# The order of the three partial products in every large matrix product of a two-layer hybrid backbone

## The chip, the core and the metric

The kernel runs on one core of one Trainium2 chip. A core has several engines with a program of their own each: TensorE (PE, matrix products; its weight loads are listed apart as PEld), VectorE (DVE), ScalarE (ACT), GpSimd (POOL) and SyncE (SP, which here starts the transfers). They meet through semaphores. The metric is the device time of one execution in microseconds, the median over several runs.

## What is computed

The reference passes 256 latent tokens and 256 context tokens of width 1024 through two layers. Layer 0 mixes with a state-space head group and a retention group that share one input and one output projection, layer 1 with an mLSTM block; each is followed by a SwiGLU feed-forward part (FFN), and the end is an RMSNorm. All in float32.

```python
def swiglu(h, w1, w3, w2):
    return (jax.nn.silu(h @ w1) * (h @ w3)) @ w2

def block_update(x, y, mod, ffn_norm_w, w1, w3, w2):
    x = x + (mod[2] * y).astype(x.dtype)
    hf = modulate(rmsnorm(x, ffn_norm_w), mod[3], mod[4])
    return x + (mod[5] * swiglu(hf, w1, w3, w2)).astype(x.dtype)
...
    for layer in range(DEPTH):
        ...
            y_l, _ = ssd_retention_mixer(h_l, rope, st, *p)
        ...
            y_l, _ = mlstm_mixer(h_l, st, *p)
        lat = block_update(lat, y_l, mod_l, norm_ffn_w[layer], ffn_w1[layer], ffn_w3[layer], ffn_w2[layer])
    return rmsnorm(lat, final_norm_w)
```

Most of the work is large products of activations (up to 512 tokens) with weight matrices: the input projections, the FFNs' three products, the mLSTM's up and down projections.

## The kernel before

TensorE multiplies tiles in the type fp32r. To keep more of float32's digits, each operand of a large product is split in two: a high part H, the operand cast to fp32r, and a low part L, what the cast left over. A product is then the sum of three partial products, high by high, high by low and low by high, accumulated in one PSUM tile.

The parts come from two engines. For a weight tile of 128x1024 SP loads wraw (L355; up to three are loaded ahead), ACT casts it to wH (L367), and VectorE subtracts to make wL (L227, the line of a helper that records every two-operand operation). wH and wL have four buffers each; `wnext` keeps up to three pairs ready. For an activation tile ACT writes hH (L499) and VectorE hL (L500); in the FFN's middle the pair is uH (L1144) and uL (L227 again). Tiles with names such as hp, hHL, uHL and yHL hold both parts in one tile, so that both read alike in a view.

`mm3` (L401) issues the partial products. It gets pairs ((lh, ll), (rh, rl)): lh and ll are the high and low part of the operand that is loaded into the array (stationary, `lhsT`), rh and rl those of the operand that streams through it (moving, `rhs`). For outputs of 512 columns it runs over two halves of 256, `CT_` and `LT_`; for each half it goes over all pairs (the 128-row slices of the contraction), and for each pair it issues three matmuls of 128x256, at L409, L410 and L411. In the trace's names `mm<-hL,wH` the moving tile stands first, the stationary one second.

Nearly everywhere the weight is stationary. In `projB`, whose output has tokens on its rows, the activation is stationary and the weight moves, so there the low moving part is wL. `mm3` is called from the first stage (L595), which makes the normalised input h slice by slice while it multiplies, from `projA` and `projB`, `out_quarter`, `tail_tiles` and `head_tiles` (FFN0 begins with several tiles at once, slice by slice), `ffn0`, `ml_qkv` (the mLSTM's blockwise projections of the convolved xc), `ztile`, `down`, and the last FFN.

Only SP's program stands in the order in which it is written. For the other engines a scheduler places the instructions by its own estimate of when their inputs and buffers are ready, so their rows can differ from the order in the source, and a changed line can move rows on engines that it doesn't name.

Of the kernel before, what the change touches and what calls it, by code (L numbers as in the profile page):

```python
# [186 lines left out]
def tile_hybrid(ctx, tc, A, out, dbg=None):  # L187
    nc = tc.nc
    V, S, G, TE = nc.vector, nc.scalar, nc.gpsimd, nc.tensor
# [14 lines left out]
    def s2(p="s2", shape=(P, 512), dt=F32):  # L204
        return sb.tile(list(shape), dt, tag="s2", name=nm(p), bufs=36)
# [195 lines left out]
    def mm3(o, pairs, first=True, last=True):  # L401

        n = len(pairs)
        if o.shape[-1] > 256:
            for sl in (CT_, LT_):
                mm3(o[:, sl], [(lp, cols(rp, sl)) for lp, rp in pairs], first and sl is CT_, last and sl is LT_)
            return
        for i, ((lh, ll), (rh, rl)) in enumerate(pairs):
            TE.matmul(o, lhsT=lh, rhs=rh, start=first and i == 0, stop=False)  # L409
            TE.matmul(o, lhsT=lh, rhs=rl, start=False, stop=False)  # L410
            TE.matmul(o, lhsT=ll, rhs=rh, start=False, stop=last and i == n - 1)  # L411

    def wk(w, k, n=P, o=0):

# [2 lines left out]
    def cols(hl, sl):  # L417
        return tuple(t[:, sl] for t in hl)
# [156 lines left out]
    for i, k in enumerate(seq):  # L575
        ld(i + 3)
        wload()
        if i < 4:
            if i > 0:
                wprep()  # L580
            w4.append(wready.pop(0))
        if i == 0:
            xn = h_a(k, rb, amix[0], ALL)
        h_b(hs[k], k, xn, mod[0][0], ALL)
        if i == 0:
            prep(1)
        prep(i + 2)
        TE.matmul(pdt[0:32, :], lhsT=wdt[:, k, :], rhs=hs[k](ALL)[0], start=i == 0, stop=False)
        TE.matmul(pdt[0:16, :], lhsT=wdt[:, k, 0:16], rhs=hs[k](ALL)[1], start=False, stop=i == KD - 1)
        if i + 1 < KD:  # L590
            fin(i + 1)
            xn = h_a(seq[i + 1], rb, amix[0], ALL)
        for j, w in enumerate(w4):
            for n in range(i + 1) if j == i else (i,):
                mm3(p4[j], [(wk(w, seq[n]), hs[seq[n]](ALL))], n == 0, n == KD - 1)  # L595
    nc.sync.dma_start(out=rowp, in_=A["rowp"][0].partition_broadcast(P))
    rl = rowp[:, RC["retl"]:RC["retl"] + 8]
# [104 lines left out]
    def projA(hs):  # L702
        w = wnext()
        p = mmps()
        for sl in (CT_, LT_) if hs[0].packed else (ALL,):
            mm3(p[:, sl], [(wk(w, k), hs[k](sl)) for k in range(KD)])
        return p

    def projB(hs, evac):
        ws = [wnext(), wnext()]  # L710
        for c in range(NCH):
            p = mmps([P, 256])
            sl = slice(c * P, (c + 1) * P)
            mm3(p, [(hs[k](sl), tuple(ws[k // 4][z][:, (k % 4) * 256:(k % 4 + 1) * 256] for z in range(2)))
                    for k in range(KD)])
            evac(c, p)
            slot()
# [705 lines left out]
    for op in order.split():  # L1423
        n = done[op] = done.get(op, -1) + 1
# [67 lines left out]
    for m in range(KD):  # L1492
        o = s2("fin")[:, :256]
# [22 lines left out]
```

## Time and profile before

| what | value |
|---|---|
| three runs | 1354.46, 1344.43, 1341.25 us |
| their median | 1344.43 us |
| the profiled execution's own time | 1343.85 us |
| its span, from the first to the last instruction | 1341.9 us |
| mean granted TensorE clock | 0.987 |
| PE / PEld / DVE / ACT / POOL busy | 1305.2 / 1250.5 / 947.8 / 642.1 / 125.0 us |

Busy time is the time in which at least one instruction of the engine ran. Matmuls are pipelined: one lasts about 0.28 us by the profile, while the next starts 0.11 to 0.12 us after it. So the time of a run of matmuls is read from the distances of their starts, or from how many a window holds. A wait belongs to the instruction that waited, and the profile names what came last for it.

### The profile page before, as it was taken

Reading aid. Unit: us, or ns where it says so; the run is one execution under the profiler, and the core shown is the slowest. Engines: PE = TensorE matmul, PEld = TensorE weight load, DVE = VectorE, ACT = ScalarE, POOL = GpSimd, SP = SyncE. Lnnn points to the kernel's source line nnn. Section 1 sums busy time; section 2 is a strip of 40 time slices with the busy share of each in tenths; the row PEclk is TensorE's granted clock in tenths of the full one; section 3 lists DMA queues with packets and bytes.
Section 4 is the critical chain, followed back from the end, with each engine's and each line's share of the span. In section 5 each row is a group of like instructions: output and inputs, shape, how many; then the busy total and the mean of one; then the engine's idle time right before and its main releaser. Section 6 shows DMA issues by size and latency. Waiting matters only on the chain.

```text
span 1341.9 us, 25691 instructions
## 1 busy us (share of the span) xinstructions
PE 1305.2 (97%) x10510; PEld 1250.5 (93%) x10510; DVE 947.8 (71%) x1703; ACT 642.1 (48%) x1114; POOL 125.0 (9%) x138
## 2 busy tenths in 40 slices
PE   7999999999999999999999999989999999999997
PEld 4899999989999999999999999989999689999997
DVE  7888787966876567897557643586666897666555
ACT  4366757846864243222322132465556563544443
POOL 0022031311021030000000310300000000000001
PEclk9999999999999999999999999999999999899998
DMA  9337344434412225567557633412124434465553
GB/s 369 111 143 236 122 162 142 134 126 152 148 48 88 80 94 188 178 237 244 190 189 249 213 95 97 140 63 63 48 65 145 138 101 146 129 206 198 194 193 122
DMA packets 60855, 201.00 MB, mean 150 GB/s; under 512 B 6841, under 2 KB 8377, under 8 KB 60737
## 3 DMA queue, kind: packets, MB, share of 16 engines
q1 hardware_dynamic: 60594, 199.36, 44.8%
q8 instruction: 82, 1.34, 0.4%
q14 instruction: 35, 0.29, 0.1%
q10 hardware_dynamic: 144, 0.01, 0.0%
HBM read 197.16 MB, written 1.13 MB: 148 GB/s over the span
## 4 chain that ended last, share of the span: by engine, by line
PE 69%; DVE 13%; issue 7%; DMA 5%; ACT 3%; POOL 1%; SPq 0%; POOLq 0%; DVEq 0%; ACTq 0%
PE mm L410 20%; PE mm L409 20%; PE mm L411 20%; DVE wL L227 3%; DVE junk L267 3%; DMA ada<-in_ada 2%; PE sc L958 1%; ACT wH L367 1%; DMA erow<-scr 1%; PE mm L1219 1%; DVE junk L291 1%; PE sc L840 1%; DVE conv L687 1%; DVE comb L227 1%; DMA wraw<-in_wup 1%
## 5 line engine op out<-in xcount | busy, mean ns | idle before, releaser
L367 ACT CAST wH<-wraw 128x1024 fp32r<-128x1024 f32 x248 | 259.4, 1048 | 408.0 <-PE mm L410 236.3
L227 DVE TENSOR_TENSOR wL<-wraw,wH 128x1024 fp32r<-128x1024 f32 x248 | 306.2, 1236 | 144.0 <-ACT wH L367 134.2
L410 PE MATMUL mm<-hL,wH 128*128 128x256 f32 x1088 | 303.1, 279 | 0.7 <-DVE hL L500 0.7
L409 PE MATMUL mm<-hH,wH 128*128 128x256 f32 x1088 | 299.5, 279 | 2.8 <-ACT hH L499 2.1
L411 PE MATMUL mm<-hH,wL 128*128 128x256 f32 x1088 | 301.8, 279 | 0.0
L409 PEld LDWEIGHTS mm<-hH,wH 128*128 128x128 f32 x1088 | 204.3, 190 | 4.5 <-ACT hH L499 2.8
L410 PEld LDWEIGHTS mm<-hL,wH 128*128 128x128 f32 x1088 | 205.7, 189 | 2.0 <-DVE hL L500 1.7
L411 PEld LDWEIGHTS mm<-hH,wL 128*128 128x128 f32 x1088 | 205.5, 189 | 0.5
L267 DVE SCALAR_TENSOR_TENSOR junk<-ada,cbc 128x1024 bf16<-128x1024 f32 x128 | 158.2, 1236 | 22.1 <-DMA ada<-in_ada 20.2
L409 PE MATMUL mm<-wH,hH 128*128 128x256 f32 x384 | 110.2, 287 | 0.2 <-ACT conv L684 0.2
L409 PE MATMUL mm<-hp,wH 128*128 128x256 f32 x384 | 108.6, 287 | 0.1
L410 PE MATMUL mm<-hp,wH 128*128 128x256 f32 x384 | 108.2, 284 | 0.0
L410 PE MATMUL mm<-wL,hH 128*128 128x256 f32 x384 | 108.0, 282 | 0.1
L411 PE MATMUL mm<-hp,wL 128*128 128x256 f32 x384 | 108.1, 283 | 0.0
L411 PE MATMUL mm<-wH,hL 128*128 128x256 f32 x384 | 107.4, 280 | 0.0
L983 DVE SCALAR_TENSOR_TENSOR xt<-mm,mod,xt 128x256 f32<-128x256 f32 x144 | 64.5, 478 | 59.3 <-PE mm L411 58.9
L687 DVE SCALAR_TENSOR_TENSOR conv<-xp,prm,conv 128x512 f32<-128x512 f32 x128 | 96.2, 754 | 12.5 <-ACT conv L684 10.9
L410 PE MATMUL mm<-uL,wH 128*128 128x256 f32 x352 | 98.2, 279 | 0.7 <-DVE uL L227 0.7
L409 PE MATMUL mm<-hHL,wH 128*128 128x256 f32 x352 | 97.6, 279 | 1.1 <-ACT hHL L499 1.1
L409 PE MATMUL mm<-uH,wH 128*128 128x256 f32 x352 | 97.8, 279 | 0.6 <-ACT uH L1144 0.6
L410 PE MATMUL mm<-hHL,wH 128*128 128x256 f32 x352 | 97.8, 278 | 0.0
L411 PE MATMUL mm<-hHL,wL 128*128 128x256 f32 x352 | 97.8, 278 | 0.0
(329 smaller groups left out, 3105.1 us busy)
## 6 DMA issues: line engine op xcount, KB each, us to landing
wraw<-in_f SPq DMA_DIRECT2D x136, 512.0 KB, 4.2
ada<-in_ada SPq DMA_DIRECT2D x80, 512.0 KB, 5.0
wraw<-in_win SPq DMA_DIRECT2D x48, 512.0 KB, 4.4
wraw<-in_wup SPq DMA_DIRECT2D x32, 512.0 KB, 3.5
erow<-scr SPq DMA_DIRECT2D x16, 512.0 KB, 7.1
wraw<-in_wout SPq DMA_DIRECT2D x16, 512.0 KB, 4.0
wraw<-in_wdn SPq DMA_DIRECT2D x16, 512.0 KB, 3.5
adaf<-in_ada SPq DMA_DIRECT2D x10, 512.0 KB, 7.6
```

Source lines behind the costliest of these rows:

```text
L227: eng.tensor_tensor(out=o, in0=a, in1=b, op=op)
L267: V.scalar_tensor_tensor(out=junk, in0=raw, scalar=1.0, in1=cbc[:, st, :], op0=ALU.mult, op1=ALU.mult, accum_out=mod[l][c][:, k, st:st + 1])
L291: V.scalar_tensor_tensor(out=junk, in0=raw, scalar=1.0, in1=cbc[:, st, :], op0=ALU.mult, op1=ALU.mult, accum_out=to)
L367: S.copy(out=H, in_=raw)
L409: TE.matmul(o, lhsT=lh, rhs=rh, start=first and i == 0, stop=False)
L410: TE.matmul(o, lhsT=lh, rhs=rl, start=False, stop=False)
L411: TE.matmul(o, lhsT=ll, rhs=rh, start=False, stop=last and i == n - 1)
L687: V.scalar_tensor_tensor(out=o, in0=x[:, :, k:k + 256], scalar=pc(wname, t * 5 + k), in1=o, op0=ALU.mult, op1=ALU.add)
L840: TE.matmul(p1[:, i, h * 64:(h + 1) * 64], lhsT=comb[(g, c0 + i)][:, h, :], rhs=xtok[:, c0 + i, h * 64:(h + 1) * 64], start=True, stop=True)
L958: TE.matmul(py[:, i, :], lhsT=src[:, i * P:(i + 1) * P], rhs=vt[:, j, :], start=j == 0, stop=j == len(srcs) - 1)
L983: V.scalar_tensor_tensor(out=xt[:, m, half], in0=p[:, o:o + 256], scalar=gate[:, m, st:st + 1], in1=xt[:, m, half], op0=ALU.mult, op1=ALU.add)
L1219: TE.matmul(pv[:, c, :], lhsT=xm[:, c0 // 2, 2 + c * P:2 + (c + 1) * P], rhs=b[:, P:], start=True, stop=True)
```

## The change

In `mm3`, the second and the third partial product change places. The first stays high by high; then comes low stationary by high moving, then high stationary by low moving. The accumulation's last matmul, which carries `stop`, is now the latter.

```diff
@@ -407,8 +407,8 @@
             return
         for i, ((lh, ll), (rh, rl)) in enumerate(pairs):
             TE.matmul(o, lhsT=lh, rhs=rh, start=first and i == 0, stop=False)
-            TE.matmul(o, lhsT=lh, rhs=rl, start=False, stop=False)
-            TE.matmul(o, lhsT=ll, rhs=rh, start=False, stop=last and i == n - 1)
+            TE.matmul(o, lhsT=ll, rhs=rh, start=False, stop=False)
+            TE.matmul(o, lhsT=lh, rhs=rl, start=False, stop=last and i == n - 1)
```

The lines keep their numbers, so L410 of before is L411 of after and the other way round. PE has as many rows as before; the scheduler moves rows on PE, ACT and VectorE beyond the exchange. Three places follow.

The first is PE's row at the head of FFN0, where four output tiles (numbers 5806, 5807, 5808 and 6021 at the end of their names) start on the first slice of h. Before:

```order
L409 MATMUL mm_829_5806<-hH_772_5587,wH_788_5603 128x256
L409 MATMUL mm_830_5807<-hH_772_5587,wH_791_5609 128x256
L409 MATMUL mm_831_5808<-hH_772_5587,wH_815_5766 128x256
L409 MATMUL mm_855_6021<-hH_772_5587,wH_818_5774 128x256
L410 MATMUL mm_829_5806<-hL_773_5588,wH_788_5603 128x256
L411 MATMUL mm_829_5806<-hH_772_5587,wL_789_5604 128x256
```

After:

```order
L409 MATMUL mm_829_5806<-hH_772_5587,wH_788_5603 128x256
L410 MATMUL mm_829_5806<-hH_772_5587,wL_789_5604 128x256
L409 MATMUL mm_830_5807<-hH_772_5587,wH_791_5609 128x256
L410 MATMUL mm_830_5807<-hH_772_5587,wL_792_5610 128x256
L409 MATMUL mm_831_5808<-hH_772_5587,wH_815_5766 128x256
L410 MATMUL mm_831_5808<-hH_772_5587,wL_816_5767 128x256
L409 MATMUL mm_855_6021<-hH_772_5587,wH_818_5774 128x256
L410 MATMUL mm_855_6021<-hH_772_5587,wL_819_5775 128x256
L411 MATMUL mm_829_5806<-hL_773_5588,wH_788_5603 128x256
```

The first matmul that reads hL was the fifth of this stretch and is the ninth. In the same way, where a part of FFN0's down product ends on its last uL, one more matmul stands ahead of it than before: line 410 of the last product, beside its line 409 and two matmuls of the next tile.

The second place is ACT's and VectorE's row at the first convolution of the mLSTM, whose result xcH feeds the blockwise projections. ACT before:

```order
L367 CAST wH_1393_10312<-wraw_1363_10132 128x1024
L682 COPY xp0_645<-mm_1365_10136 128x2x256
L684 ACTIVATE conv_1386_10292<-mm_1365_10136,prm_68 128x512
L682 COPY xp1_646<-mm_1366_10137 128x2x256
L367 CAST wH_1415_10428<-wraw_1364_10134 128x1024
```

ACT after:

```order
L682 COPY xp0_645<-mm_1365_10136 128x2x256
L684 ACTIVATE conv_1386_10292<-mm_1365_10136,prm_68 128x512
L367 CAST wH_1393_10312<-wraw_1363_10132 128x1024
L682 COPY xp1_646<-mm_1366_10137 128x2x256
L367 CAST wH_1415_10428<-wraw_1364_10134 128x1024
```

VectorE at the same place, before:

```order
L227 TENSOR_TENSOR wL_1394_10313<-wraw_1363_10132,wH_1393_10312 128x1024
L687 SCALAR_TENSOR_TENSOR conv_1386_10292<-xp0_645,prm_68,conv_1386_10292 128x512 x2
L227 TENSOR_TENSOR wL_1416_10429<-wraw_1364_10134,wH_1415_10428 128x1024
L687 SCALAR_TENSOR_TENSOR conv_1386_10292<-xp0_645,prm_68,conv_1386_10292 128x512
L227 TENSOR_TENSOR gm_10278<-mm_1404_10388,rowp_69 128x32
L687 SCALAR_TENSOR_TENSOR conv_1386_10292<-xp0_645,prm_68,conv_1386_10292 128x512
```

VectorE after:

```order
L687 SCALAR_TENSOR_TENSOR conv_1386_10292<-xp0_645,prm_68,conv_1386_10292 128x512 x2
L227 TENSOR_TENSOR wL_1394_10313<-wraw_1363_10132,wH_1393_10312 128x1024
L687 SCALAR_TENSOR_TENSOR conv_1386_10292<-xp0_645,prm_68,conv_1386_10292 128x512
L227 TENSOR_TENSOR gm_10278<-mm_1404_10388,rowp_69 128x32
L687 SCALAR_TENSOR_TENSOR conv_1386_10292<-xp0_645,prm_68,conv_1386_10292 128x512
```

The cast of the weight tile has moved behind the copy and the first tap of the convolution on ACT; on VectorE the first wL has moved behind two further taps, and the second (10429, further down) behind all of them.

The third place is VectorE's row in the second head of the mLSTM's scan, where earg (12078, 12096) is scaled at L1331 before PE reads it at L1338. Before:

```order
L1329 RECIPROCAL rr_1672_12082<-rr_1672_12082 128x2
L227 TENSOR_TENSOR rr_1677_12100<-rr_1677_12100,den_1674_12091 128x2
L1318 ISA earg_1699_12208,negm_1696_12202<-urow_1695_12199,mmask_1382_10283 128x512
L1318 ISA negm_1696_12202 128x1
L1329 RECIPROCAL rr_1677_12100<-rr_1677_12100 128x2
L227 TENSOR_TENSOR wL_1712_12272<-wraw_1688_12158,wH_1711_12271 128x1024
L1331 SCALAR_TENSOR_TENSOR earg_1671_12078<-earg_1671_12078,rr_1672_12082,earg_1670_12074 128x512
```

After:

```order
L1329 RECIPROCAL rr_1677_12100<-rr_1677_12100 128x2
L1318 ISA earg_1699_12208,negm_1696_12202<-urow_1695_12199,mmask_1382_10283 128x512
L1318 ISA negm_1696_12202 128x1
L1331 SCALAR_TENSOR_TENSOR earg_1671_12078<-earg_1671_12078,rr_1672_12082,earg_1670_12074 128x512
L1321 SCALAR_TENSOR_TENSOR earg_1698_12204,den_1697_12203<-earg_1698_12204,S_1539_11242 128x512
L1331 SCALAR_TENSOR_TENSOR earg_1676_12096<-earg_1676_12096,rr_1677_12100,earg_1675_12092 128x512
```

wL_1712_12272 no longer stands ahead of the first L1331; it comes some ten rows behind it. On PE the matmul that reads earg_12078 has moved forward too: of the matmuls of lines 409 to 411 for tile 12277, ten follow it now, where two followed it before.

## Rows read from the trace of the kernel before

**Rows 1.** The page, part 1: busy us (share of the span) x instructions.

```profile
PE 1305.2 (97%) x10510; PEld 1250.5 (93%) x10510; DVE 947.8 (71%) x1703; ACT 642.1 (48%) x1114; POOL 125.0 (9%) x138
```

**Rows 2.** The page, part 4: the chain that ended last, shares by engine.

```profile
PE 69%; DVE 13%; issue 7%; DMA 5%; ACT 3%; POOL 1%; SPq 0%; POOLq 0%; DVEq 0%; ACTq 0%
```

**Rows 3.** Windows: us, busy (x instructions) by engine, granted clock, DMA share, GB/s.

```profile
585.20:715.20 130.00, 130.00 (x1150) 130.00 (x1149) 89.28 (x146) 33.47 (x40) 0.00 (x0) 1.00 0.62 211
716.00:828.00 112.00, 112.00 (x952) 111.98 (x952) 58.95 (x88) 27.99 (x35) 14.50 (x16) 1.00 0.49 163
1154.00:1332.00 178.00, 178.00 (x1573) 178.00 (x1572) 106.56 (x136) 84.13 (x118) 5.16 (x5) 1.00 0.56 181
490.00:503.00 13.00, 12.61 (x95) 12.41 (x96) 12.34 (x30) 5.97 (x14) 0.94 (x2) 0.87 0.30 116
```

**Rows 4.** The page, part 5: weight loads by line; busy, mean ns, then idle before.

```profile
L409 PEld LDWEIGHTS mm<-hH,wH 128*128 128x128 f32 x1088 | 204.3, 190 | 4.5 <-ACT hH L499 2.8
L410 PEld LDWEIGHTS mm<-hL,wH 128*128 128x128 f32 x1088 | 205.7, 189 | 2.0 <-DVE hL L500 1.7
```

**Rows 5.** Line 410: its idle time by releaser, and who waited for it (us, times).

```profile
  DVE hL L500: 2.4, 6
  DVE uL L227: 2.0, 5
  DVE wL L227: 0.3, 1
...
  ACT wH L367: 236.3, 105
```

**Rows 6.** Timeline of PE at 491 and 715 us: start, duration, then idle before.

```profile
491.03 0.70 PE L409 MATMUL mm<-hH,wH 128*128 128x256 f32 x4
492.01 0.58 PE L410 MATMUL mm<-hL,wH 128*128 128x256 f32 x1 [0.28 <-DVE hL L500]
...
715.30 0.28 PE L410 MATMUL mm<-uL,wH 128*128 128x256 f32 x1
715.78 0.38 PE L410 MATMUL mm<-uL,wH 128*128 128x256 f32 x1 [0.21 <-DVE uL L227]
```

**Rows 7.** Timeline of PE in the middle of FFN0's second down product.

```profile
750.87 0.28 PE L409 MATMUL mm<-uH,wH 128*128 128x256 f32 x1
750.99 0.28 PE L410 MATMUL mm<-uL,wH 128*128 128x256 f32 x1
751.10 0.28 PE L411 MATMUL mm<-uH,wL 128*128 128x256 f32 x1
751.22 0.28 PE L409 MATMUL mm<-uH,wH 128*128 128x256 f32 x1
751.34 0.28 PE L410 MATMUL mm<-uL,wH 128*128 128x256 f32 x1
```

**Rows 8.** Timelines of ACT, DVE and PE before the mLSTM's first blockwise product.

```profile
879.14 1.05 ACT L367 CAST wH<-wraw 128x1024 fp32r<-128x1024 f32 x1 [1.54 <-PE mm L410]
...
880.22 1.23 DVE L227 TENSOR_TENSOR wL<-wraw,wH 128x1024 fp32r<-128x1024 f32 x1 [2.10 <-ACT wH L367]
...
882.85 1.22 DVE L227 TENSOR_TENSOR wL<-wraw,wH 128x1024 fp32r<-128x1024 f32 x1
...
887.22 0.39 PE L409 MATMUL mm<-xcH,bH 128*128 128x256 f32 x1 [4.31 <-ACT xcH L1200]
887.44 0.40 PE L1229 MATMUL sc<-xcH,ghl 128*32 128x512 f32 x1
887.95 0.58 PE L410 MATMUL mm<-xcL,bH 128*128 128x256 f32 x1
```

**Rows 9.** Timelines of DVE and PE in the mLSTM scan's second head.

```profile
1041.98 1.21 DVE L227 TENSOR_TENSOR wL<-wraw,wH 128x1024 fp32r<-128x1024 f32 x1
1043.11 1.41 DVE L1331 SCALAR_TENSOR_TENSOR earg<-earg,rr,earg 128x512 f32<-128x512 f32 x2
...
1044.00 0.63 PE L1338 MATMUL sc<-cst,earg 128*128 128x128 f32 x4 [2.30 <-DVE earg L1331]
```

## Prediction, made before the changed kernel ran

> **What bounds the kernel now.** I read the engines' busy shares first. TensorE (PE) is busy 97% of the span, and it executes as many weight loads (PEld) as matmuls, 10510 each [rows 1]; VectorE follows with 71%. The chain of work that ended last says the same: 69% of it is PE [rows 2]. So the time is a count of matmuls times their spacing, plus the short stretches in which PE stands still, and a change that only permutes matmuls can act on the spacing or on the stretches.
>
> For the spacing I read windows in which PE never idles. From 585.2 to 715.2 us 1150 matmuls take 130 us, 113.0 ns each, and from 1154 to 1332 us 1573 take 178 us, 113.2 ns each. From 716 to 828 us, with the same granted clock of 1.00 and matmuls of the same shape, 952 take 112 us, 117.6 ns each [rows 3]. The reader should see two cadences at one clock, 4.5 ns apart, and that a cadence, once there, lasts over a thousand matmuls. No row tells what selects it; the slower stretch begins right behind a short stop at 715.78 us [rows 6].
>
> For the stops I read what PE waited for ahead of line 410, which before the change is the first matmul to need a low moving operand: 2.4 us in 6 waits for hL and 2.0 us in 5 for uL [rows 5]. No line 411 had a wait of that size, since whatever it needs was made before. The two largest stops elsewhere that touch rearranged code are 4.31 us for xcH [rows 8] and 2.30 us for earg [rows 9].
>
> **The change, part by part.** It adds and removes no instruction: 9408 matmuls of lines 409 to 411, counted in the program (a third each, 3136), stay, and their weight loads with them.
>
> *The kept stationary.* Before, lines 409 and 410 use one stationary twice running; after, no two neighbours of a triple share it (line 411 returns to the first). If the second load had been cheap, 3136 cheap loads would be lost. The loads' mean times are 190 ns at line 409 and 189 at line 410, where the same tile is loaded again [rows 4], and a run of five matmuls has steps of 0.12 and 0.12 into line 410, 0.11 into line 411, and 0.12 into line 409 [rows 7]: the step that repeats the stationary is not the shorter one. Cost taken: 0. Bounds: the loads differ by 1 ns, so 3136 x 1 ns = 3.1 us of loss at most by these rows; a gain of the same size isn't excluded.
>
> [...]
>
> *Waits for low parts.* The wait moves from the second matmul of a triple to the third, so one more matmul (0.113 us) runs ahead of it. At the last part of each FFN0 down product PE stops for uL, as at 715.78 us, where the step from the matmul ahead is 0.48 us instead of 0.11 [rows 6]. Ahead of that wait stood, after the triple before, line 409 of the last product and lines 409 and 410 of the next tile; now line 410 of the last product stands there too. Three such places: 3 x 0.113 = -0.34 us. At FFN0's head four matmuls of line 409 ran, and then PE waited for hL (492.01 against 491.03 us) [rows 6]; now eight run ahead of it. Four matmuls of cover: 4 x 0.113 = -0.45 us. At the first mLSTM qkv product xcL came 0.51 us after the matmul ahead of it [rows 8], and now one product of that triple and twelve of the next tile stand ahead of it: about -0.25 us, nearly all of what that step has over the one before it (0.51 - 0.22 = 0.29). The bounds for the three: 0, and all 4.4 us of waits for hL and uL [rows 5] gone. I take the direct count, since in stage one, where the other hL waits lie, the program puts as many matmuls between hH and the first use of hL as before.
>
> *Earlier use of wL, later release of wH.* wL is now needed one matmul sooner and wH is held one matmul longer (0.113 us). Work that hides it: weight pairs are made up to three tiles ahead. Ahead of line 410 PE waited for wL once, 0.3 us, while ACT's cast of wH waited for line 410 in 105 cases, 236.3 us in all [rows 5]: the casts wait for PE to free buffers, not PE for the casts. Cost 0; without that cover 0.113 us for each of the program's 248 casts, 28 us, would be the price, but this needs weights that arrive late, and the windows of the FFNs with no idle PE [rows 3] show none.
>
> *What the scheduler moves on ACT and VectorE.* Because a wH buffer now comes free only with a tile's very last matmul, ACT's reader of that tile moves ahead of the cast of the next wH. At the first mLSTM convolution ACT's cast (879.14 us, 1.05) and VectorE's two wL (880.22 us, 1.23, and 882.85 us, 1.22) ran ahead of or inside the convolution on which xcH depends [rows 8]. After, the copy and the convolution come first, and one wL is left between the steps. The chain shortens by the cast's 1.05 us, not by the sum, since the taps still follow each other; PE's wait of 4.31 us becomes about 3.26. Term: -1.05 us, bounds 0 (if another input of xcH is then last) and -2.3 (one wL more).
>
> At the mLSTM scan's second head VectorE's wL at 1041.98 us stood ahead of earg at 1043.11, 1.13 us later [rows 9]; after, it stands behind. But the matmul that reads earg also moved forward, by eight matmuls, which now run behind it (8 x 0.113 = 0.90 us). Net -0.23 us, bounds +0.9 (earg not earlier) and -1.13.
>
> **The sum.** -0.34 -0.45 -0.25 -1.05 -0.23 = -2.3 us on the profiled execution's 1343.85 us gives 1341.5. The median of the runs shown, 1344.43, is 0.6 us above that execution, so on medians 1342.1; I say 1342.0. With the bounds: gains of at most 4.4 + 2.3 + 1.1 = 7.8 us, losses of at most 3.1 + 0.9 = 4.0 us.
>
> **Rivals.**
> (a) The cadence turns long, the case on the other side. Its place: the two stretches at 113 ns, 1150 and 1573 matmuls [rows 3], each entered behind a stop whose matmul the change replaces. Its price: (1150 + 1573) x 4.5 ns = 12.3 us, so 1342 + 12.3 = 1354; the longer stretch alone 7.1 us, 1349. For it: such a stretch follows a stop directly, and every stop is rearranged. Against it: only one of three long stretches had it. Slower than before by over 1% (13.4 us) it decides only from 13.4 / 0.0045 = about 2980 matmuls on, so all of these and some of the short ones.
> (b) The cadence turns short from 716 to 828 us: 952 x 4.5 ns = 4.3 us, 1337.7. For it: that stretch's stop is shortened by one matmul; against it: nothing tells what selects it.
> (c) The kept stationary did save something: +3.1 us, 1345. Against it: equal loads and steps [rows 4, 7]. [...]
> [...]
> (e) The stops only move: whatever ends a wait ends the next at the same time, and nothing changes, 1344.4.
>
> **How the numbers follow.** The forecast (1338 to 1346, its own range, and it includes e) has 0.60; (a) 0.18, of which 0.06 reach past 1%; (b) 0.12, of which 0.04 come with so much of the waits' upper bound, 1342 - 4.3 - 5.3 = 1332 and below, that it is about 1%; (c) 0.04; (d) 0.06. The range for 8 in 10 goes from 1334 (b with part of the larger gains) to 1352 (a with its longer stretch and (d)'s wait). About 1% is what a measurement of this kernel can tell from no change: the limits are 1331.0 and 1357.9 us. Faster by more 0.05, within 0.88, slower by more 0.07.
>
> **What would show it.** Steps between starts of 113 or 117.6 ns in the same windows as before, equal for all three lines, show the cost of the kept stationary right at 0; a step into line 410 or 411 that is longer than the others shows (c). Idle ahead of line 411 for uL, three times about 0.1 us less, and hL at FFN0's head about 0.45 us less show the moved waits; a wait for xcH of about 3.3 us shows the reordered casts; 4.3 says that ACT's row wasn't its cause. Matmuls per window in the three long stretches tell (a) and (b). The prediction is wrong in its main point if steps in a stretch at full clock differ by line, or if PE gains idle of more than 4 us ahead of lines 409 to 411.

## The result and the profile after

The changed kernel is slower: 1348.96 us, the median of 20 runs (1343.63 to 1361.32), against 1341.83 us for the kernel before (20 runs, 1335.23 to 1354.46). The ratio is 1.0066, with a 95% interval of 1.0044 to 1.0088, so some 6 to 12 us were lost where 2.3 were to be gained. The ratios here and below come from the fast executions alone (those not over 1.5% above the fastest of the same kernel), and differ by up to 0.2% from the quotient of the two medians. The time lies inside the range for 8 in 10 (1334 to 1352), but above the forecast's own (1338 to 1346) and on the wrong side of the kernel before, and the loss has a cause that the sum didn't hold.

First the page of the changed kernel: part 1 (busy us, share, instructions), and from part 5 the weight loads of the three lines (busy, mean ns, then idle before).

```profile
PE 1316.3 (97%) x10510; PEld 1264.4 (93%) x10510; DVE 946.9 (70%) x1703; ACT 644.0 (47%) x1116; POOL 131.1 (10%) x138
...
L409 PEld LDWEIGHTS mm<-hH,wH 128*128 128x128 f32 x1088 | 205.1, 189 | 4.5 <-ACT hH L499 3.4
L410 PEld LDWEIGHTS mm<-hH,wL 128*128 128x128 f32 x1088 | 206.1, 189 | 0.4
L411 PEld LDWEIGHTS mm<-hL,wH 128*128 128x128 f32 x1088 | 204.4, 189 | 0.8 <-DVE hL L500 0.4
```

There is still one load for each matmul, and the loads of these groups last 189 ns at all three lines, as in [rows 4]. What the change does to TensorE's own work costs nothing that these rows show.

The waits of PE in the changed kernel (total us, times, longest) show something new at the top:

```profile
PE mm L411 <- DVE wL L227: 6.5, 3, 4.0
PE mm L409 <- ACT xcH L1200: 3.7, 1, 3.7
...
PE sc L1338 <- DVE earg L1331: 2.3, 2, 1.9
...
PE mm L411 <- DVE uL L227: 0.3, 1, 0.3
...
PE mm L411 <- DVE hL L500: 0.2, 1, 0.2
```

PE now waits 6.5 us for wL, where no matmul of the kernel before waited for one (the 0.3 us of [rows 5] is a weight load's). The waits that I had worked out did shrink: xcH from 4.31 to 3.7 us [rows 8], earg's longest from 2.30 to 1.9 [rows 9], and little is left of those for uL and hL. They are all smaller than the new one.

Here is the longest of the new stops, in the timeline of PE (start, duration, then idle before):

```profile
216.48 0.28 PE L411 MATMUL mm<-wL,hH 128*128 128x256 f32 x1
217.09 0.38 PE L409 MATMUL mm<-wH,hH 128*128 128x256 f32 x1 [0.33 <-ACT wH L367]
217.31 0.28 PE L410 MATMUL mm<-wH,hL 128*128 128x256 f32 x1
221.58 0.58 PE L411 MATMUL mm<-wL,hH 128*128 128x256 f32 x1 [4.00 <-DVE wL L227]
221.96 0.42 PE L409 MATMUL mm<-wH,hH 128*128 128x256 f32 x1
222.18 0.42 PE L410 MATMUL mm<-wH,hL 128*128 128x256 f32 x1
222.39 0.41 PE L411 MATMUL mm<-wL,hH 128*128 128x256 f32 x1
```

The names say which product this is: wH and wL stand first, so the weight moves. It is one of `projB`'s, in layer 0's mixing stage. Each of its products takes two weight tiles, and PE stands at the first low matmul of the second tile. Behind the stop the steps are 0.21 us instead of 0.11. VectorE and ACT in the same stretch show what was late:

```profile
217.06 0.74 DVE L728 SCALAR_TENSOR_TENSOR yL<-sc,prm,yH 128x512 fp32r<-128x512 f32 x1
217.73 1.40 DVE L687 SCALAR_TENSOR_TENSOR conv<-xp,prm,conv 128x512 f32<-128x512 f32 x2
219.05 0.68 DVE L227 TENSOR_TENSOR comb<-erow 128x512 f32<-128x512 f32 x1
219.65 0.74 DVE L687 SCALAR_TENSOR_TENSOR conv<-xp,prm,conv 128x512 f32<-128x512 f32 x1
220.31 1.22 DVE L227 TENSOR_TENSOR wL<-wraw,wH 128x1024 fp32r<-128x1024 f32 x1
...
213.82 1.28 ACT L757 ACT_TABLE_LOAD   x1
215.12 0.40 ACT L757 ACTIVATE erow<-erow,ncs 128x128 f32<-128x128 f32 x1
215.43 0.67 ACT L727 ACTIVATE yH<-sc,prm 128x512 fp32r<-128x512 f32 x1
216.00 1.03 ACT L367 CAST wH<-wraw 128x1024 fp32r<-128x1024 f32 x1
```

The cast of that tile ran on ACT at 216.00 us, behind the mixer's own rows, and PE's matmul at 217.09 waited 0.33 us for it. The subtraction was then ready to run, but VectorE had five other instructions in front of it (yL, three convolution taps, comb) and never idled. In the kernel before the same two instructions ran 8.5 and 9.1 us earlier, far ahead of PE, which reached this product at 217.05 us and didn't stop:

```profile
207.49 1.04 ACT L367 CAST wH<-wraw 128x1024 fp32r<-128x1024 f32 x1
...
211.24 1.22 DVE L227 TENSOR_TENSOR wL<-wraw,wH 128x1024 fp32r<-128x1024 f32 x1
```

The second stop has the same form, at another product of `projB`, 2.33 us. It is followed a little later by twelve matmuls of line 822 that take 4.44 us, where they took 2.75 before:

```profile
373.62 0.28 PE L410 MATMUL mm<-wH,hL 128*128 128x256 f32 x1
376.22 0.38 PE L411 MATMUL mm<-wL,hH 128*128 128x256 f32 x1 [2.33 <-DVE wL L227]
...
377.50 4.44 PE L822 MATMUL sc<-vw,btok 128*128 128x256 f32 x12
```

The windows (us; busy and instructions of PE, PEld, DVE, ACT, POOL; granted clock; DMA share; GB/s) price both, first of the kernel before, then of the changed one:

```profile
200.00:230.00 30.00, 29.18 (x254) 28.76 (x254) 25.36 (x37) 20.21 (x34) 2.48 (x2) 1.00 0.39 119
360.00:382.00 22.00, 22.00 (x186) 21.69 (x185) 19.60 (x35) 11.85 (x23) 0.00 (x0) 1.00 0.33 112
```

```profile
200.00:230.00 30.00, 25.68 (x199) 25.28 (x199) 23.47 (x31) 24.18 (x38) 4.00 (x4) 0.89 0.42 135
360.00:382.00 22.00, 19.67 (x147) 18.67 (x146) 19.98 (x33) 13.46 (x22) 0.00 (x0) 0.92 0.40 126
...
221.90:226.00 4.10, 4.10 (x20) 4.10 (x20) 4.10 (x7) 3.21 (x5) 0.00 (x0) 0.50 0.38 128
...
378.00:380.00 2.00, 2.00 (x7) 1.56 (x6) 1.75 (x4) 0.73 (x2) 0.00 (x0) 0.50 0.74 225
```

PE starts 55 and 39 matmuls fewer in these stretches, and the granted clock falls from 1.00 to 0.89 and 0.92. It is 0.50 in the windows behind the two stops, from 221.9 to 226.0 and from 378.0 to 380.0 us.

To follow the loss through the program, I compare the start of the same matmul of line 409 (counted from 0) in both traces. Number 406 (213.65 us before) starts 1.82 us earlier after the change and number 438 starts 5.89 us later, so the first stop costs 7.7 us. The rows give nearly all of it: the step into line 411 is 4.27 us instead of 0.11 (4.16), the one into line 409 ahead of it 0.61 (0.50), and the stretch at half clock holds 20 matmuls in 4.10 us and about 14 in the next 2 (4.10 + 2.00 - 34 x 0.113 = 2.3), with 0.27 for the step from 221.58 us. Numbers 758 to 790 span the second stop: from 2.75 to 7.25 us late, 4.5 us, of which 2.49 is the step and 4.44 - 2.75 = 1.69 line 822. Between the two 3.1 us are given back, in part by smaller waits (for `vw` 0.3 us instead of 0.8, for `zs` none instead of 0.6). By number 1014 (485 us before), the end of the mixing stage, the changed kernel is 7.2 us late.

Most of what this one execution (1358.5 us, 14.65 above the one of before) loses beyond that is cadence. These are the windows of the changed kernel that answer to [rows 3]:

```profile
593.54:718.00 124.46, 124.46 (x1058) 124.46 (x1058) 82.78 (x137) 30.12 (x36) 0.00 (x0) 1.00 0.60 199
729.60:838.00 108.40, 108.39 (x955) 108.20 (x955) 58.80 (x89) 27.96 (x35) 14.68 (x16) 1.00 0.52 168
1163.00:1338.00 175.00, 175.00 (x1488) 175.00 (x1487) 101.34 (x126) 79.37 (x111) 1.92 (x2) 1.00 0.58 183
...
490.00:503.00 13.00, 11.89 (x103) 11.67 (x102) 9.44 (x20) 6.17 (x12) 4.56 (x6) 1.00 0.34 121
```

That is 117.6, 113.5 and 117.6 ns per matmul, where [rows 3] had 113.0, 117.6 and 113.2: all three long stretches have changed sides. By the numbers, (1150 + 1573 - 952) x 4.4 ns = +7.8 us. At FFN0's head 1.1 us came back (the clock is now 1.00 there); FFN0's first stretch ran at 117.8 ns instead of 113.4 and lost 2.8; the mLSTM, where three of the forecast's terms lie, gave back 2.7. 7.2 + 7.8 - 1.1 + 2.8 - 2.7 = 14.0 us; number 3100, near the end, is 13.9 us late. Whether the cadence belongs to the change is for the experiments.

### The profile page after: what moved, and what is told of

It is laid out like the page before. It is cut to its first block, busy times and chain, and to the rows that moved or that the text cites. A ratio compares the mean times of both kernels' runs of the same rounds, so it can differ in the third digit from the quotient of the medians.

```text
span 1356.7 us, 25632 instructions
## 1 busy us (share of the span) xinstructions
PE 1316.3 (97%) x10510; PEld 1264.4 (93%) x10510; DVE 946.9 (70%) x1703; ACT 644.0 (47%) x1116; POOL 131.1 (10%) x138
## 4 chain that ended last, share of the span: by engine, by line
PE 68%; DVE 13%; issue 8%; DMA 4%; ACT 4%; POOL 2%; SPq 0%; POOLq 0%; DVEq 0%; ACTq 0%
PE mm L411 20%; PE mm L409 20%; PE mm L410 20%; DVE wL L227 3%; DMA erow<-scr 2%; DVE junk L267 2%; DVE conv L687 2%; PE sc L958 1%; DMA ada<-in_ada 1%; ACT wH L367 1%; PE mm L1219 1%; DVE junk L291 1%; PE sc L822 1%; PE sc L840 1%; DVE comb L227 1%
## 5 line engine op out<-in xcount | busy, mean ns | idle before, releaser
L409 PE MATMUL mm<-hH,wH 128*128 128x256 f32 x1088 | 304.5, 281 | 2.7 <-ACT hH L499 2.7
L410 PE MATMUL mm<-hH,wL 128*128 128x256 f32 x1088 | 303.2, 279 | 0.0
L411 PE MATMUL mm<-hL,wH 128*128 128x256 f32 x1088 | 300.5, 279 | 0.2 <-DVE hL L500 0.2
L410 PEld LDWEIGHTS mm<-hH,wL 128*128 128x128 f32 x1088 | 206.1, 189 | 0.4
L411 PEld LDWEIGHTS mm<-hL,wH 128*128 128x128 f32 x1088 | 204.4, 189 | 0.8 <-DVE hL L500 0.4
L411 PE MATMUL mm<-wL,hH 128*128 128x256 f32 x384 | 109.1, 285 | 6.5 <-DVE wL L227 6.5
L410 PE MATMUL mm<-wH,hL 128*128 128x256 f32 x384 | 108.7, 283 | 0.0
L410 PE MATMUL mm<-hp,wL 128*128 128x256 f32 x384 | 107.6, 282 | 0.0
L411 PE MATMUL mm<-hp,wH 128*128 128x256 f32 x384 | 106.8, 283 | 0.0
L409 PE MATMUL mm<-hHL,wH 128*128 128x256 f32 x352 | 100.4, 285 | 1.1 <-ACT hHL L499 1.1
L410 PE MATMUL mm<-hHL,wL 128*128 128x256 f32 x352 | 100.1, 284 | 0.0
L411 PE MATMUL mm<-hHL,wH 128*128 128x256 f32 x352 | 99.6, 284 | 0.0
L411 PE MATMUL mm<-uL,wH 128*128 128x256 f32 x352 | 97.8, 279 | 0.5 <-DVE uL L227 0.3
```

The costliest lines, as they stand in the source:

```text
L410: TE.matmul(o, lhsT=ll, rhs=rh, start=False, stop=False)
L411: TE.matmul(o, lhsT=lh, rhs=rl, start=False, stop=last and i == n - 1)
```

## The experiments

The theories. A: the order of the matmuls itself costs nothing; the loss is in ACT's and VectorE's rows, which the scheduler rearranged, above all in the two late weight pairs of the mixing stage. B: the matmul order itself costs time (the kept stationary, or the cadence that goes with it). C: the loss is in the FFNs or the mLSTM, by their moved waits. Each ratio below stands against the kernel before, run on the same chip in turn.

### e1: the two late pairs back in front

New order; the cast and subtraction of the two late tiles get a higher priority.

```diff
@@ wprep, from the changed kernel
-        S.copy(out=H, in_=raw)
-        tt(V, L, raw, f32v(H), ALU.subtract)
+        with tc.high_priority(offset=400) if wno[0] in (27, 49) else nullcontext(): S.copy(out=H, in_=raw); tt(V, L, raw, f32v(H), ALU.subtract)
+        wno[0] += 1
```

> The changed kernel, with two weight tiles of the scan stage (the second tile of two token-major products, wL_2545 and wL_4355) given a higher priority, so that ACT casts and VectorE subtracts them where they stood before the change. Theory 1 (these two tiles, made late, are the loss): PE's waits for wL of 4.0 and 2.3 us vanish, with them the half-clock stretch behind the first; the time falls by 6 to 8 us against the changed kernel, ratio to the kernel before 0.999 to 1.002. Theory 2 (the new order draws the longer cadence, 117.6 ns instead of 113.2, more often): ratio stays near 1.006, with no wait for wL. Theory 3 (the kept stationary saved load time): ratio stays near 1.006, and the steps between matmuls differ by line.

Measured: 1347.09 us against 1342.19, ratio 1.0035 (1.001 to 1.006). Both stops are gone: matmul 438 is as early as 406 was, and at 1014 the kernel is 0.8 us late instead of 7.2. But the price of one pair moved forward is another row moved back, here `zs` on ACT, for which PE waited 0.6 us before (waits of PE):

```profile
PE mm L409 <- ACT zs L774: 2.7, 1, 2.7
```

The ratio lies above the 0.999 to 1.002 that A gave. By the two ratios about half of the loss goes with the two pairs, but their intervals overlap. What the rest is, this run doesn't say.

### e2: the two pairs late, in the old order

Old order; only these two tiles' cast and subtraction are tied behind the instructions that they follow in the changed kernel.

```diff
@@ from the kernel before
-        S.copy(out=H, in_=raw)
-        tt(V, L, raw, f32v(H), ALU.subtract)
+        mark[uid[0] - 1] = S.copy(out=H, in_=raw), tt(V, L, raw, f32v(H), ALU.subtract)
...
+    for w, j, to in ((376, 0, (368, 'y')), (376, 1, (374, 1)), (606, 0, (605, 3)), (606, 1, (601, 4))):
+        tc.add_manual_dep(mark[w][j].ins, mark[to].ins.name, mybir.DependencyInfo(mybir.DependencyClass.NoSync, mybir.DependencyReason.DATA), reason="late")
```

> The kernel before, its order of partial products untouched, with only these two weight tiles made late: on ACT and VectorE their cast and subtraction stand behind the same rows as in the changed kernel. Theory 1: PE waits for wL about 4 and 2.3 us in the scan stage, the time is 6 to 8 us above the kernel before, ratio 1.0045 to 1.006. Theories 2 and 3: ratio 0.999 to 1.001, since no matmul moves.

Measured: 1354.62 us, ratio 1.0096 (1.0064 to 1.0127). The old order now has the stop, at line 410 and of the same length:

```profile
PE mm L410 <- DVE wL L227: 4.9, 2, 4.2
...
PE mm L409 <- ACT uH L1144: 4.2, 1, 4.2
```

Matmul 438 is 6.3 us later relative to 406, and at 1014 the kernel is 7.2 us late. Two tiles out of 248 are enough for a loss of at least the size of the change's, with all but twelve of PE's 10510 rows where they were. The ratio lies above the forecast 1.0045 to 1.006, though the second stop is only 0.67 us here, not 2.3. The second line is a wait at the end of FFN0's first part, which ran from none to 5.2 us over the profiles, in either order of the matmuls; here VectorE waited 3.7 us for a transfer of `ada` before it. It may have a part in this run's loss.

### e3 and e4: the new order in one half of the program

A switch in `mm3` gives the new order only up to FFN0 (e3) or only from FFN0 on (e4).

```diff
@@ mm3 and ffn0, from the changed kernel; e4 has False and True exchanged
-    wraws = []
+    wraws, sw = [], [True]
...
-            TE.matmul(o, lhsT=ll, rhs=rh, start=False, stop=False)
-            TE.matmul(o, lhsT=lh, rhs=rl, start=False, stop=last and i == n - 1)
+            TE.matmul(o, lhsT=ll if sw[0] else lh, rhs=rh if sw[0] else rl, start=False, stop=False)
+            TE.matmul(o, lhsT=lh if sw[0] else ll, rhs=rl if sw[0] else rh, start=False, stop=last and i == n - 1)
...
-        ps = head_tiles(nrm, 3)
+        sw[0] = False; ps = head_tiles(nrm, 3)
```

> The new order up to the end of the mixer of layer 0, the old one from FFN0 on. Theory 1: all of the loss, +6 to +8 us, ratio 1.005 to 1.006, with waits for wL of 4.0 and 2.3 us. Theories 2 and 3: the loss goes by the number of matmuls, about 3,500 of 9,408 lie here, so +3 us, ratio 1.002 to 1.0025.

> The old order up to the end of the mixer of layer 0, the new one from FFN0 on, so in both FFNs and the mLSTM. Theory 1: no loss, -2 to +1 us by the shortened waits, ratio 0.998 to 1.001. Theories 2 and 3: the larger part of the loss, about +5 us, ratio 1.004; in theory 2 the long stretches of the FFNs run at 117.6 ns, in theory 3 one of the three steps is longer.

Measured: e3 1352.1 us, ratio 1.0086 (1.0055 to 1.0117), with the waits for wL of the changed kernel (6.6 us, 3 times, longest 4.0). e4 1340.03 us, ratio 0.9992 (0.9967 to 1.0018), without them. So C falls: two FFNs and the mLSTM in the new order cost nothing that shows, and the loss comes with the part before FFN0. (By the trace 3072 matmuls of the three lines lie there, not 3,500; for B the difference is small.) The gains of the forecast lie in e4's half; they are too small for the interval.

### e5 and e6: order of the matmuls and rows of the other engines, crossed

The decisive pair. Each instruction of ACT, VectorE and GpSimd is tied to its predecessor in a list: in e5 the new matmul order runs with the other engines' rows of the kernel before, in e6 the old matmul order with the rows of the changed kernel. In the traces ACT's and VectorE's rows are those of the list one for one, and PE's are those of the kernel with the same matmul order in all but 173 (e5) and 220 (e6) of 10510 places.

```diff
@@ end of the program; the list differs between e5 and e6
+    _chain(tc)
...
+def _chain(tc):
...
+    for rows in ORDER.values():
...
+        for x, y in zip(names, names[1:]):
+            tc.add_manual_dep(by[y], x, mybir.DependencyInfo(mybir.DependencyClass.NoSync, mybir.DependencyReason.DATA), reason="chain")
```

> The new order of the partial products on PE, while every instruction of ACT, VectorE and GpSimd is chained to stand in the order that it had before the change (issue order only, no wait added). Theory 1, widened (the loss is what the scheduler did to ACT's and VectorE's order in the scan stage, not the order of the matmuls): ratio 0.998 to 1.001, no wait for wL above 0.6 us, as the kernel before. Theories 2 (longer cadence) and 3 (kept stationary): ratio about 1.006, since the matmuls are those of the changed kernel.

> The opposite: the old order of the partial products, with ACT, VectorE and GpSimd chained to the order of the changed kernel. Theory 1, widened: ratio 1.005 to 1.010, with waits for wL of about 4 and 2.3 us. Theories 2 and 3: ratio 0.999 to 1.001.

Measured: e5 1343.51 us against 1344.03, ratio 0.9995 (0.9969 to 1.0021). e6 1351.81 us, ratio 1.0079 (1.0045 to 1.0114). The window around the first stop, of e5 and then of e6 (columns as above), with e6's wait:

```profile
200.00:230.00 30.00, 29.71 (x255) 29.49 (x254) 25.10 (x36) 20.26 (x34) 2.48 (x2) 1.00 0.40 122
```

```profile
200.00:230.00 30.00, 25.60 (x209) 25.21 (x209) 23.65 (x32) 23.87 (x38) 4.16 (x4) 0.94 0.40 132
...
221.76 0.58 PE L410 MATMUL mm<-wL,hH 128*128 128x256 f32 x1 [4.11 <-DVE wL L227]
```

New matmuls with old rows start 255 matmuls there, as the kernel before (254). Old matmuls with new rows start 209 and stop for 4.11 us; the second stop is 1.07 us here. The time follows the rows of ACT, VectorE and GpSimd, and not the order of the matmuls: A stands as to the rows, B falls. How much of the loss is the two stops, these two runs don't divide.

### e7 and e8: all weight pairs in front

If late pairs are the fault, could all pairs go first? Every cast and subtraction gets a moderate priority, in the new order (e7) and in the old one (e8).

```diff
@@ wprep
-        S.copy(out=H, in_=raw)
-        tt(V, L, raw, f32v(H), ALU.subtract)
+        with tc.high_priority(offset=100) if True else nullcontext(): S.copy(out=H, in_=raw); tt(V, L, raw, f32v(H), ALU.subtract)
```

> The changed kernel with every weight tile's cast and subtraction raised by 100 places in the scheduler's priority. If late weights alone are the loss: ratio 0.997 to 1.001 and no wait for wL above 0.6 us. If the readers of finished tiles, which now come later, are as sensitive (the wait for zs of 2.7 us that stood in the run with two early tiles): other waits take its place, ratio 1.002 to 1.006.

> The kernel before with the same raised priority of all weight tiles. If its order of ACT and VectorE was already a good one: ratio 0.999 to 1.004, other waits growing. If it is a better one: below 0.998, by shorter waits in the scan stage.

Measured: e7 1352.02 us, ratio 1.0045 (1.0015 to 1.0076); e8 1356.37 us, ratio 1.0101 (1.006 to 1.0142). It is no cure: e7 lies within its 1.002 to 1.006, e8 far above its 0.999 to 1.004, and in the old order it loses as much as the late pairs did. In e8 no wait for wL is left among the large ones, but others have come up (waits of PE):

```profile
PE sc L1338 <- DVE rr L227: 4.3, 2, 2.4
...
PE mm L409 <- ACT conv L684: 1.6, 1, 1.6
...
PE mm L409 <- ACT qkraw L880: 1.4, 1, 1.4
```

The weight pairs and the mixers share ACT and VectorE. Whichever goes first, the other's row is late for PE at some place.

### e9 and e10: one stop at a time

The list of e5, for instructions 1900 to 3300 alone (around the first stop, e9) or 3300 to 5200 alone (around the second, e10), in the new order.

```diff
@@ as in e5, from the changed kernel; ORDER holds only that part
+    _chain(tc)
```

> The changed kernel, with ACT, VectorE and GpSimd chained to their old order only for the instructions emitted around the first stop for wL (roughly 165 to 300 us, wL_1895 to wL_3180); all else is free and stands as in the changed kernel, the late wL_4355 among it. If the loss is made at the two stops, and mostly at the first: PE's wait of 4.0 us at 222 us is gone, the one of 2.3 us at 376 us stays; ratio 1.001 to 1.004. If the loss is spread over many rows: ratio stays above 1.005.

> The same for the instructions emitted around the second stop (roughly 300 to 480 us, wL_3357 to wL_5158); the late wL_2545 stays as in the changed kernel. If the loss is made at the two stops: the wait of 2.3 us at 376 us is gone, the one of 4.0 us at 222 us stays with the half-clock stretch behind it; ratio 1.004 to 1.007. If it is spread: about the same as the run before.

Measured: e9 1346.07 us against 1341.16, ratio 1.0029 (1.0002 to 1.0055); e10 1351.84 us, ratio 1.0071 (1.0042 to 1.0101). Waits of PE for wL, in e9 and then in e10:

```profile
PE mm L411 <- DVE wL L227: 1.1, 2, 0.9
```

```profile
PE mm L411 <- DVE wL L227: 4.2, 2, 4.0
```

In e9 the first stop is gone, the second shrinks by itself to 0.92 us, and line 822 behind it takes 2.75 us again. In e10 the first stop remains, the second is gone. The first is the dear one, as its 7.7 of the 12.2 us in the traces said.

The traces and the times side by side. "First" and "second" are how much later matmul 438 is relative to 406, and 790 relative to 758; "stage's end" is the lateness of matmul 1014; all in us against the trace of the kernel before.

| kernel | first | second | stage's end | ratio |
|---|---|---|---|---|
| changed kernel | 7.7 | 4.5 | 7.2 | 1.0066 |
| e2 old order, two pairs late | 6.3 | 1.2 | 7.2 | 1.0096 |
| e6 old order, new rows | 6.5 | 1.6 | 4.1 | 1.0079 |
| e3 new order before FFN0 | 6.5 | 2.9 | 4.2 | 1.0086 |
| e10 second stop's rows old | 6.9 | 0.9 | 4.6 | 1.0071 |
| e9 first stop's rows old | 0.0 | 1.4 | -0.1 | 1.0029 |
| e1 two pairs early | 0.0 | 0.0 | 0.8 | 1.0035 |
| e5 new order, old rows | 0.4 | 0.0 | -1.1 | 0.9995 |
| e4 new order from FFN0 on | 0.0 | 0.0 | -3.0 | 0.9992 |

Of these, every kernel with the first stop loses 0.7 to 1.0%, every one without it at most 0.35%. That stop is not the only way to lose: e7 and e8 don't have it, are 4.2 and 5.0 us late at the stage's end, and lose 0.45 and 1.0%. (By matmul number 150, at 103 us, traces already differ from that of before by -0.9 to +1.3 us, so a single figure of the last column but one is good to about 1 us.) One thing stays open: nearly all ratios say some us more than the lateness at the stage's end (e2: 12.9 against 7.2; e9: 3.9 against -0.1). One trace stands there against many runs, and the next section shows how much the cadence can add to one execution; the traces settle no more than that.

### e11: the cadence

Nearly all long stretches of the profiles start at one of two spacings and keep it. I count the matmuls of lines 409 to 411 in unbroken runs of twelve or more steps that average over 115 ns: some 2800 of about 9100 in the kernel before and 5400 in the changed one, but in e1, with every row of PE as in the changed kernel, 2700, and in e5 2100. For the last FFN this is e9, with PE's rows of the changed kernel and 113.1 ns per matmul, beside that kernel's 117.6 above:

```profile
1156.00:1331.00 175.00, 175.00 (x1547) 175.00 (x1546) 104.74 (x132) 81.98 (x115) 5.42 (x5) 1.00 0.58 184
```

The same sequence of matmuls runs at either spacing, so the order of the matmuls alone doesn't choose it. Whether the rows of the other engines make the long one more frequent is open. The other profiles with the first stop have 2600 (e3), 4000 (e2), 5200 (e6, in the old order) and 6300 (e10); those without it 3100 (e4), 3600 (e9), 2900 (e8) and 5300 (e7). But this is one profile for each kernel, and those with many are also executions far above their kernel's median (the changed kernel 1358.5 against 1349.0 us, e10 1360.5 against 1351.8), so a part of the rows' cost may be cadence, and one trace each doesn't tell.

Some places nearly always chose alike: behind a group of line 797 it was the short one in 39 of 40 cases, four in each of the ten profiles up to e8. e11 puts four unused matmuls of another kind behind FFN0's and the last FFN's stops, in the old order.

```diff
@@ from the kernel before
+    def dum(H, L):
+        p = scps()
+        for c in range(4):
+            TE.matmul(p[:, c * P:(c + 1) * P], lhsT=f32v(L)[:, (c % 2) * P:(c % 2 + 1) * P], rhs=f32v(H)[:, (c % 2) * P:(c % 2 + 1) * P], start=True, stop=True)
...
+                if m == 2:
+                    dum(*h2[0](CT_))
...
```

> The kernel before, with up to four float32 matmuls of 128x128 without use put behind the stops of both FFNs (FFN0's head, the first tile of each of its down products, the last FFN's head), to see whether what stands ahead of a long stretch selects its cadence. In the scan such a group (L797) was followed by the shorter cadence 39 times in 40. If the group selects it: all six long stretches at about 113 ns. If a cadence is drawn at each restart whatever stands ahead: a mixture again, as in the runs so far, where about 4 of 10 matmuls stood in the longer one. Time: 4 us more for the added matmuls, and up to 13 us less.

Measured, one time: 1347.92 us, beside 1341.16, the median of the kernel before on that chip. Windows of two of FFN0's stretches and of the last FFN, and the added group in the latter's timeline (eight rows for its four matmuls):

```profile
600.00:710.00 110.00, 110.00 (x973) 110.00 (x972) 70.77 (x111) 29.38 (x36) 0.00 (x0) 1.00 0.59 204
735.00:830.00 95.00, 94.97 (x836) 94.68 (x836) 44.08 (x68) 25.23 (x33) 13.75 (x16) 1.00 0.48 157
1165.00:1325.00 160.00, 160.00 (x1361) 160.00 (x1361) 92.91 (x116) 72.15 (x100) 0.96 (x1) 1.00 0.60 190
...
1159.09 1.05 PE L416 MATMUL sc<-hHL 128*128 128x128 f32 x8
```

That is 113.1, 113.6 and 117.6 ns. All four stretches of FFN0 behind an added group (595, 1124, 923 and 197 matmuls) were short; but FFN0's stretches were all short in e1 and e5 too, without it. In the last FFN the scheduler had placed the group 79 matmuls into the stretch: the spacing was 117.8 ns ahead of it and 117.8 ns for the 1486 matmuls behind it. So such a group doesn't by itself select the short spacing, and a choice made at the restart fits, but one execution is no proof. Nor did it pay: no gain shows in the one time. No run here was clearly faster than the kernel before.

## Why the prediction was wrong, point by point

**What bounds the kernel** was right: PE 97%, and what moves the time is stops and spacing. The base was high: 1344.43 us from three runs, 1341.83 from 20, so that 1342.0 meant a gain of 2.4 us and would have been none.

**The kept stationary, cost 0**: right. Loads of 189 ns in all three lines, and e5 (new order, old rows) at 0.9995. Both traces have 10510 loads for 10510 matmuls, before [rows 1] and after.

**Waits for low parts**: right in kind, in size only at uL. A stop for uL at an end of FFN0's down product has a step of 0.38 us, where it was 0.48 [rows 6], so 0.10 for the 0.113 worked out. At FFN0's head, line 411's first matmul follows at 0.11 us and no wait for hL is left; the clock stayed at 1.00 there, where it had been 0.87 [rows 3], which the sum had not counted, so 1.1 us came back instead of 0.45. Two readings were wrong. The bound of 4.4 us added the idle of the weight loads to that of the matmuls; PE's own waits of the kernel before were 1.4 us:

```profile
PE mm L410 <- DVE hL L500: 0.7, 2, 0.4
PE mm L410 <- DVE uL L227: 0.7, 2, 0.5
```

And the step of 0.51 us ahead of xcL was for the most part no wait: the matmul in front of it has 512 columns (line 1229), and line 1230, as wide, also took 0.43 us, from its start at 888.54 us to the next at 888.97. So little of the -0.25 us was there to gain; in the changed kernel xcL is read without a wait.

**The scheduler's moves at xcH and earg**: right in direction. The wait for xcH fell by 0.62 us of the 1.05 forecast (4.31 to 3.69); earg's longest wait fell by 0.4 us, where 0.23 was forecast.

**"Earlier use of wL, later release of wH", cost 0**: this is the step that failed, for two reasons. First, I argued from averages of the kernel before: casts waited 236.3 us for PE, so PE doesn't wait for casts [rows 5]. That slack belonged to the row order of the kernel before. In the changed kernel it is smaller, and with the new matmul order and the old rows (e5) it is nearly what it was, as line 411's lists of those who waited for it show (us, times; the changed kernel, then e5):

```profile
  ACT wH L367: 166.8, 68
```

```profile
  ACT wH L367: 229.1, 98
```

Secondly I priced the change of the need, one matmul or 0.113 us, and not the change of the place. In `projB` the weight moves, so there wL is needed a matmul later, and it is there that PE stopped: the need shifted by 0.1 us one way, the subtraction by 9 us. The "windows of the FFNs with no idle PE" named as evidence were the wrong stage. In the mixing stage ACT and VectorE serve the convolution, the state-space head group and the weights together. What the runs showed in place of the cost of 0: two stops for wL of 4.00 and 2.33 us, 7.7 and 4.5 us in the trace with what follows them, and with the rows alone exchanged (e6) a loss of 0.8%.

**The choice of places.** "What the scheduler moves on ACT and VectorE" was worked out at two places, both in the mLSTM, since there known stops would shrink. Looking only where a stop already was finds the gains. The losses stood in rows of the mixing stage where PE had not waited before, and these could be read off beforehand: in the changed kernel's row of VectorE that wL stands ten rows further back, the one of the second stop nineteen.

**The rivals.** The chances give 0.06 to a (d), and the range adds its wait to (a): a stop of PE at a row of the mLSTM's scan, for earg. No run shows that term; the longest wait for earg fell from 2.30 to 1.9 us. In its place the runs showed a new stop in another stage, the 4.00 us for wL, which cost 7.7 us with the granted clock at 0.50 from 221.9 to 226.0 us behind it. (a) and (b), the cadence, both show in the profile of the changed kernel; the order of the matmuls doesn't choose them, since other kernels with the same order had the other spacing, but whether the moved rows make the long one more frequent is open. (c) did not happen. The range held by luck: it reached 1352 for the cadence, not for late weights. My criterion, "idle of more than 4 us ahead of lines 409 to 411", is met by line 411's 6.5 us for wL.

## What to carry to other kernels

Where a scheduler places the work, a change of a few matmuls is a change of every engine's rows: compare the rows of all engines over the whole program, and check each producer that has moved back against the time at which its reader needs it, above all where there was no wait before. Slack read as a total ("the casts wait for PE") doesn't protect the one tile that comes late; here the stop of 4.00 us cost 7.7, some 2.6 us of it (2.3 + 0.27) in the stretch at half clock behind it (granted clock 0.50). To tell whether an order of instructions costs by itself or by what it does to the others, cross the two, as e5 and e6 do.

## What the runs showed of the hardware that was not expected

Equal matmuls at a granted clock of 1.00 run at 113 or 117.6 ns each, and a stretch keeps its spacing for up to 1573 matmuls [rows 3]. The same sequence had either in different profiles (the last FFN in the new order: 117.6 in the changed kernel, 113.1 in e9), and four matmuls of another kind in the middle of a long stretch left it at 117.8 ns (e11). At 4.4 ns over the 2600 matmuls that the changed kernel had more in long stretches (5400 against 2800) this is by my estimate 11 us, so that it can account for much of the scatter of a kernel's runs (1335 to 1354 us for the kernel before). What decides it stays open.

Behind the stop of 4.00 us the granted clock was 0.50 for at least 4.1 us; behind that of 2.33 us the steps stayed at 0.11 to 0.12 for a microsecond, and the half clock showed only from shortly before 378 us on, 1.2 us or more behind the stop (0.80 from 377 to 378 us, 0.50 from 378 to 380).
